# A two-layer sequence encoder on one core: weight sums and product adds pinned to traced order, PSUM banks dealt anew

## The chip, the core and the metric

The kernel runs on one core of a Trainium2 chip. Five engines of that core take part, each with its own in-order stream of instructions: TensorE (PE, matrix products, with its weight loads shown apart as PEld), VectorE (DVE), ScalarE (ACT), GpSimd (POOL) and SyncE (SP, which here only issues transfers). They meet through semaphores alone: an instruction whose operand isn't there holds up everything behind it on its engine. ACT has two jobs here: it computes, and it issues the transfers of the weight sums, from the same stream. Matrix products go to PSUM, eight banks of 128 partitions by 512 fp32 values.

The metric is the device time of one execution in microseconds (us); lower is better. Times of a comparison are medians of several runs.

## The reference

One sequence of 16 learned meta tokens and 256 frames, width 2048, goes through two post-norm layers:

```python
for layer in range(DEPTH):                       # DEPTH = 2
    f = _even_mixer(h, ...) if layer % 2 == 0 else _odd_mixer(h, ...)
    h = _layer_norm(DEEPNORM_ALPHA * h + f, ln_g[layer], ln_b[layer])
return h[:, PREFIX:]
```

The even mixer projects h (2048 wide) to queries, keys, values and gates of four gated-linear-attention (GLA) heads and eight stick-breaking attention heads, runs both, multiplies with SiLU gates and projects the 3072 columns back to 2048. The odd mixer is a Mamba-2 block: an input projection to z (4096), x (4096), B and C (1024 each) and 64 step sizes; a causal convolution of four taps and a SiLU on x, B, C; a scan in eight groups; an RMS norm per group of 512 columns; and the output projection of 4096 to 2048 columns. All weights and results are fp32.

## The kernel before

**Products.** Every large fp32 product is computed as three products of fp32r parts: a weight tile is split into whi (a rounding copy on ACT, line 191) and wlo (weight minus whi, a subtraction on DVE or sometimes POOL, line 192), and the activations into xhi and xlo. Lines 214, 215 and 216 are the three matmuls whi by xhi, whi by xlo and wlo by xhi.

**Units.** The weights are cut into units of 128 partitions by 2048 columns (1 MB), in the order of two lists, L0 (104 units of layer 0) and L1 (of layer 1). SP loads them into three buffers, raw. An input unit (in_unit) is 16 row blocks of three matmuls into one PSUM bank of the name pj, in four quarters of 12 matmuls; its result is then read out by a post function of its kind. In quarters 0 and 2 half of the next unit is split. Layer 0 goes through GLA heads 0 to 3, with output units between, then the two quads of stick-breaking heads. Layer 1 goes through the groups 0 to 7, each with the ten units B, C, x (four) and z (four). The first three units of layer 0 run interleaved while their data arrives; the ticks (below) begin after them.

**Side tasks.** Everything that isn't a unit is a Python generator: gates, transposes through DRAM, the mixers, the weight sums. After each quarter, tick() lets each waiting generator take one step. So the order in which the program is traced is the order of the units with the steps of the side tasks strewn in by ticks.

**Who sets the order on the chip.** The traced order is not the final one. A planner simulates the program and deals each engine its instructions: among those whose predecessors are through in its simulation, the one of highest priority, which follows the traced order, except that the post functions and some adds are traced with a high priority. It may thus issue an instruction much earlier than it stands in the trace, when its operands are there early. `keep_in_program_order` adds one edge: the instruction is issued behind the instruction that was traced just before it on its own engine. It is an edge of issue order, with no wait on a semaphore. Several matmul groups are pinned that way already; and the end of layer 0 and of the kernel are kept in traced order on DVE and ACT (keep_order).

**Weight sums.** The output projection of groups 0 to 5 in layer 1 uses a scheme of seven products of 2x2 blocks in place of eight (SEVEN). It needs four sums of weight blocks for each of 12 block sets, and these depend on weights alone, so they are computed during layer 0 by two generators (quad_sums, lines 560 to 582). Each of the 48 blocks of work loads 0.5 MB of weights into one of two buffers, quad (line 571, issued by ACT), lets 7 ticks pass, does four subtractions in place on DVE (line 575), lets 2 ticks pass, stores the result to DRAM (line 580, issued by ACT, tensor qs), and lets 4 ticks pass. The two generators start 12 and 19 ticks after the ticks begin and take every other block.

**Products of layer 1.** From quarter 72 of layer 1 on, 14 products per group are strewn between the quarters of the units (product, lines 615 to 637): six matmuls of 512 columns each (line 630) into one of two accumulator banks, then one add of the bank into acc on DVE (line 634). The add is put off to the next product_step, a quarter later. Its weights come through praw (SP) and lines 191 and 192. The products 0, 2, 4 and 6 of a set of seven use accumulator 0, the others accumulator 1.

**PSUM.** Eight banks: pj0 to pj3, po (two in rotation), z0 and z1. In layer 0 and the first six units of layer 1 the in-units rotate through all four pj banks; after that `self.pjs = (0, 1)`, and pj2 and pj3 are the product accumulators. z0 and z1 hold the score matrices of the mixers (zbank() deals them in turn), the means and scales of the first layer norm, and in layer 1 per group the small product cb of C and B (decay1, lines 1263 to 1274) and four small transposes (x_path). po serves short outputs: diagonal outputs of the scan (two), the mean square, x's transposes (two).

Of the kernel before, what the change touches and what calls it, by code (L numbers as in the profile page):

```python
# [117 lines left out]
class _Body:  # L118
# [114 lines left out]
    def run(self):  # L233
        tc, nc = self.tc, self.nc
        with tc.tile_pool(name="cp", bufs=1) as cp, tc.tile_pool(name="wp", bufs=1) as wp, tc.tile_pool(
            name="pp", bufs=1, space=PSUM
        ) as pp:
            self.cp, self.wp, self.pp = cp, wp, pp
            self.raw, self.parts = {}, {}
            self.zb = [pp.tile([P, 512], F32, tag=f"z{i}", name=f"z{i}") for i in range(2)]  # L240
            self.zi = 0

            self.dta = cp.tile([64, 2], F32, tag="dta", name="dta")
            self.b_one, self.b_rms, self.b_ln = [cp.tile([P, 1], F32, tag=n, name=n) for n in ("b_one", "b_rms", "b_ln")]
            self.xrows = [cp.tile([P, KT, XW], F32R, tag=n, name=n) for n in ("xhi", "xlo")]
            self.xhi, self.xlo = [x[:, :, X0 : X0 + T] for x in self.xrows]
            self.setup()
            with tc.tile_pool(name="hp", bufs=1) as hp:
                self.hp = hp
                a = hp.tile([P, HPG * 416], F32, tag="hacc", name="hacc")[:, : 12 * T].rearrange("p (k t) -> p k t", t=T)  # L250
                self.hacc = _TwoTiles(a, hp.tile([P, 4, T], F32, tag="hacc2", name="hacc2"))
                with tc.tile_pool(name="l0", bufs=1) as lp:
                    self.lp = lp
                    self.layer0()
                with tc.tile_pool(name="l1", bufs=1, reuse_waits="tile") as lp:
                    self.lp = lp
                    self.layer1()
# [301 lines left out]

    def quad_sums(self, start, first):  # L560

        nc, sub = self.nc, self.nc.vector.tensor_tensor
        for _ in range(start):
            yield
        for m in range(first, 8 * NS7, 2):
            g, q, c, x = m // 8, m // 4 % 2, m // 2 % 2, m % 2
            if (g, q) not in self.sums:
                self.sums[g, q] = self.tc.dram_tile([2, P, 2048], F32, name=self.nm("qs"))
            part = lambda a: a[c].rearrange("p (s x) -> p s x", s=4)[:, :, x * 256 : (x + 1) * 256]
            b = self.lp.tile([P, 4, 256], F32, tag="quad", name=self.nm("quad"), bufs=2)  # L570
            nc.scalar.dma_start(b, part(self.quad_rows(g, q)))
            for _ in range(7):
                yield
            for n, (o, u, v) in enumerate(((0, 1, 0), (1, 2, 1), (2, 2, 0), (3, 2, 3))):
                sub(b[:, o, :], b[:, u, :], b[:, v, :], op=ALU.subtract)  # L575
                if n % 2:
                    yield
            for _ in range(2):
                yield
            nc.scalar.dma_start(part(self.sums[g, q]), b)  # L580
            for _ in range(4):
                yield

# [31 lines left out]
    def product(self, k):  # L615

        mm = self.nc.tensor.matmul
        g, q, n = PRODUCTS[k]
        name, _, _, bank, first, (t, c) = SEVEN[n]
        while name not in self.left[g]:  # L620
            self.tick()
        yh, yl = self.left[g][name]
        hi, lo = [a.rearrange("p (k c) -> p k c", k=2) for a in self.pparts.pop(k)]
        if first and (n < 2):
            self.pbank[bank] = self.bank(2 + bank)
        ps = self.pbank[bank]
        f = first
        for j in range(2):
            for a, b in ((yh, hi), (yh, lo), (yl, hi)):
                mm(ps, a[:, j, :], b[:, j, :], start=f, stop=(j == 1 and a is yl), skip_group_check=True)  # L630
                f = False
        dq = 2 * q + c
        a = self.acc[:, t, dq * 512 : (dq + 1) * 512]
        self.padd = lambda: self.nc.vector.tensor_tensor(a, a, ps, op=ALU.add)  # L634
        self.pdone = k + 1
        self.product_load(k + 3)
        self.product_split(k + 1)
# [176 lines left out]

    def zbank(self):
        self.zi ^= 1
        return self.zb[self.zi]

    def mix_tile(self, g):
        lp = self.lp  # L820
# [229 lines left out]
    def layer1(self):  # L1050
        nc, lp = self.nc, self.lp
        self.acc = lp.tile([P, 2, D], F32, tag="acc", name="acc")
        self.praw, self.pparts, self.pbank = {}, {}, {}
        self.left_tiles = {n: [self.left_tile(a, k, t) for a in n] for n, k, t in LEFT}
        self.mt = lp.tile([16, HPG, 16], F32, tag="mt", name="mt")


        self.mt2 = lp.tile([48, 4, 2, 16], F32, tag="mt2", name="mt2")
        self.xd2 = lp.tile([48, 4, 64], F32, tag="xd2", name="xd2")
        nc.vector.memset(self.mt2, 0.0)  # L1060
        nc.vector.memset(self.xd2, 0.0)
        self.rstd1 = {}
        self.first1()
        self.pjs = (0, 1)
        self.units(len(L0), L1[:-5], {n: None for n in range(NFIRST)})
        self.tail()

# [156 lines left out]
    def decay1(self, g):  # L1224
        nc, lp = self.nc, self.lp
        act, vec, mm = nc.scalar.activation, nc.vector, nc.tensor.matmul
        bc = self.cur["bc", g]
        self.silu1(bc, None if g else vec)
        yield
        if g:  # L1230
            yield from _wait(*self.mixers[6 + g - 1])
        else:
            yield from _wait(self.tasks["dt"], self.tasks["res"])
            self.load_decay(0)
            yield
            yield
        if g > 1:
            bch, bcl = [a for a in lp.tile([P, 2, T + S], F32R, tag="gz", name=self.nm("bcp")).rearrange("p a c -> a p c")]
            act(bch, bc, AF.Copy)
            vec.tensor_tensor(bcl, bc, bch.bitcast(F32), op=ALU.subtract)  # L1240
            pairs = ((bch, bch), (bch, bcl), (bcl, bch))
        else:
            pairs = ((bc, bc),)

        M = lp.tile([P, HPG, 400], F32, tag="M", name=self.nm("M"))
        self.cur["M", g] = M
        eb = self.cur["ebc", g]
        for h in range(HPG):
            gh = g * HPG + h
            for s, c in ((0, slice(0, 256)), (1, slice(256, 400))):  # L1250
                act(M[:, h, c], eb[:, h, c], AF.Relu, bias=self.est[:, 0, s, gh : gh + 1], scale=-1.0)  # L1251
            if h % 2:
                act(M[:, h - 1 : h + 1, :], M[:, h - 1 : h + 1, :], AF.Exp, scale=-1.0)
                yield
        mt = self.mt
        e2 = self.est2[:, 0, g * HPG : (g + 1) * HPG].rearrange("p (h o) -> p h o", o=1).broadcast_to([16, HPG, 16])
        vec.tensor_tensor(mt, eb[:16, :, 400:416], e2, op=ALU.subtract)
        vec.tensor_scalar(mt, mt, 0.0, None, op0=ALU.min)
        act(mt, mt, AF.Exp)
        yield  # L1260

        for _ in range(2 if g else 0):
            yield
        zb = self.zbank()
        pin = self.tc.keep_in_program_order
        for o, s0, n, t0 in ((zb[:, 16:272], 0, P, 0), (zb[:, 272:416], P, P, 112), (zb[:16, 0:16], 2 * P, NM, 240)):
            for i, (b, c) in enumerate(pairs):
                pin(mm(o, b[:, s0 : s0 + n], c[:, T + t0 :], start=i == 0, stop=i == len(pairs) - 1))
        yield
        cb = lp.tile([P, 416], F32, tag="cb", name=self.nm("cb"))  # L1270
        act(cb, zb[:, :416], AF.Copy)
        self.causal(cb[:, 16:128], 112, False, 16)
        self.causal(cb[:, 272:400], 128, False)
        self.causal(cb[:16, 0:16], 16, False)
        yield
        for h in range(0, HPG, 2):
            c = cb[:, 16:416].rearrange("p (o c) -> p o c", o=1).broadcast_to([P, 2, 400])
            vec.tensor_tensor(M[:, h : h + 2, :], M[:, h : h + 2, :], c, op=ALU.mult)
            yield
        c = cb[:16, 0:16].rearrange("p (o c) -> p o c", o=1).broadcast_to([16, 2, 16])  # L1280
        m = mt.rearrange("s (p j i) t -> s j p i t", j=2, i=2)
        for j in range(2):
            for p in range(2):
                vec.tensor_tensor(self.mt2[32 * j : 32 * j + 16, 2 * p : 2 * p + 2, j, :], m[:, j, p], c, op=ALU.mult)
        yield
# [391 lines left out]
```

## Time and profile before

| what | value |
|---|---|
| time, median of 3 runs | 1498.27 us (1496.67 to 1498.56) |
| the profiled execution's own time | 1493.46 us |
| its span, first to last instruction | 1491.7 us |
| mean granted TensorE clock | 0.977 |
| PE, DVE, ACT, POOL busy | 94%, 76%, 56%, 18% |
| layer 0 | about 0 to 785 us |
| products of layer 1 | about 890 to 1415 us |

A row of the profile names line, engine, operation, output tile <- input tiles, count, and busy time with the mean of one. A row of a view of waits says which engine and line waited for which engine (or DMA) and line, how many us in total, how many times and the longest. PEclk or "clock" is the share of full clock that TensorE was granted. Idle time of an engine that isn't the bottleneck costs nothing by itself.

### The profile page before, as it was taken

To read this page: it belongs to the slowest core of one execution; us is meant where nothing else is said; L and a number is where in the kernel's file an instruction comes from. 1 tells how busy PE (TensorE), PEld (TensorE's weight loads), DVE (VectorE), ACT (ScalarE), POOL (GpSimd) and SP (SyncE) were. 2 spreads that over 40 slices of the span, in tenths; PEclk is the share of its full clock that TensorE was granted. 3 is DMA by queue.
4 is the path that set the end of the run, shared out by engine and by line. 5 is a ranking of instruction groups with operands and counts; after the bars stand their busy time and mean duration, and the time that the engine had idled before them with its cause. 6 is when DMAs were issued, how large, how long until landed. Compare 5 with 4: busy or idle time off the path is not lost.

```text
span 1491.7 us, 26723 instructions
## 1 busy us (share of the span) xinstructions
PE 1399.3 (94%) x10559; PEld 1335.1 (89%) x10559; DVE 1137.7 (76%) x1924; ACT 842.8 (56%) x1299; POOL 269.4 (18%) x269
## 2 busy tenths in 40 slices
PE   6898979989989999999998989999999999999998
PEld 6798979989988999999998989888988989988986
DVE  5867658678667567456888877987879798787977
ACT  4444424434434554455568777668675776858661
POOL 0001000000000110001610131233224223222241
PEclk8899998999999999999999999999999999999999
DMA  9778877887986545554535647666576666756551
GB/s 313 245 262 274 266 252 236 289 284 261 304 273 210 177 158 181 177 175 157 170 141 188 232 174 244 226 214 243 184 250 214 227 233 215 240 179 229 187 198 57
DMA packets 132029, 325.97 MB, mean 219 GB/s; under 512 B 28672, under 2 KB 80704, under 8 KB 106560
## 3 DMA queue, kind: packets, MB, share of 16 engines
q1 hardware_dynamic: 80496, 273.15, 54.2%
q10 hardware_dynamic: 51408, 51.12, 10.3%
q8 instruction: 83, 1.36, 0.4%
q14 instruction: 42, 0.34, 0.1%
HBM read 293.33 MB, written 30.91 MB: 217 GB/s over the span
## 4 chain that ended last, share of the span: by engine, by line
PE 57%; DMA 16%; DVE 16%; issue 5%; ACT 5%; POOL 1%; ACTq 1%; DVEq 0%; SPq 0%; POOLq 0%
PE pj L214 15%; PE pj L216 15%; PE pj L215 15%; DMA qs<-quad 7%; DMA quad<-in_wts 6%; DVE wlo L192 6%; PE pj L630 5%; DVE quad L575 2%; ACT whi L191 2%; PE po L1435 1%; DMA raw<-in_wts 1%; ACT M L1251 1%; DVE xt L1195 1%; DVE acc L634 1%; PE po L754 1%
## 5 line engine op out<-in xcount | busy, mean ns | idle before, releaser
L214 PE MATMUL pj<-xhi,whi 128*128 128x272 f32 (+4 forms) x2560 | 740.0, 290 | 14.9 <-DVE bc L1195 5.6
L215 PE MATMUL pj<-xlo,whi 128*128 128x272 f32 (+4 forms) x2560 | 736.9, 288 | 7.0 <-DVE xlo L369 6.8
L216 PE MATMUL pj<-xhi,wlo 128*128 128x272 f32 (+4 forms) x2560 | 735.9, 288 | 5.3 <-DVE wlo L192 5.1
L191 ACT ACTIVATE whi<-raw 128x1024 fp32r<-128x1024 f32 (+2 forms) x386 | 395.4, 1033 | 315.6 <-PE pj L215 162.6
L192 DVE TENSOR_TENSOR wlo<-raw,whi 128x1024 fp32r<-128x1024 f32 (+2 forms) x365 | 443.4, 1220 | 156.4 <-ACT whi L191 155.4
L214 PEld LDWEIGHTS pj<-xhi,whi 128*128 128x128 f32 x2560 | 487.5, 191 | 24.8 <-issue 7.7
L215 PEld LDWEIGHTS pj<-xlo,whi 128*128 128x128 f32 x2560 | 487.9, 191 | 11.6 <-DVE xlo L369 7.0
L216 PEld LDWEIGHTS pj<-xhi,wlo 128*128 128x128 f32 x2560 | 488.3, 191 | 6.7 <-DVE wlo L192 5.9
L575 DVE TENSOR_TENSOR quad<-quad 128x256 f32<-128x256 f32 x192 | 85.5, 460 | 49.7 <-DMA quad<-in_wts 48.4
L214 PE MATMUL pj<-mixh,whi 128*128 128x272 f32 x384 | 114.9, 300 | 3.7 <-DVE hacc L489 2.7
L192 DVE TENSOR_TENSOR wlo<-praw,whi 128x1024 fp32r<-128x1024 f32 x84 | 110.3, 1314 | 8.1 <-ACT whi L191 8.0
L215 PE MATMUL pj<-mixl,whi 128*128 128x272 f32 x384 | 113.5, 296 | 0.0
L216 PE MATMUL pj<-mixh,wlo 128*128 128x272 f32 x384 | 113.1, 295 | 0.0
L191 ACT ACTIVATE whi<-praw 128x1024 fp32r<-128x1024 f32 x84 | 88.5, 1053 | 30.8 <-PE pj L215 17.1
L634 DVE TENSOR_TENSOR acc<-acc,pj 128x512 f32<-128x512 f32 x84 | 57.1, 679 | 38.7 <-PE pj L630 38.6
L214 PEld LDWEIGHTS pj<-mixh,whi 128*128 128x128 f32 x384 | 75.4, 197 | 4.9 <-DVE hacc L489 3.4
L299 POOL TENSOR_TENSOR gr<-gr,gsc 128x1088 f32<-128x1088 f32 x6 | 16.3, 2724 | 346.8 <-ACT gsc L298 259.6
L215 PEld LDWEIGHTS pj<-mixl,whi 128*128 128x128 f32 x384 | 75.6, 197 | 0.2
L216 PEld LDWEIGHTS pj<-mixh,wlo 128*128 128x128 f32 x384 | 75.4, 196 | 0.0
L192 POOL TENSOR_TENSOR wlo<-raw,whi 128x1024 fp32r<-128x1024 f32 x21 | 56.2, 2674 | 99.3 <-ACT whi L191 99.3
L1251 ACT ACTIVATE M<-ebc,est 128x256 f32<-128x256 f32 (+1 forms) x128 | 46.1, 448 | 19.3 <-PE po L1435 18.9
L1206 POOL TENSOR_TENSOR gz<-gz,xcl 128x512 f32<-128x512 f32 x16 | 27.2, 1703 | 110.9 <-ACT xcl L1205 96.5
(395 smaller groups left out, 1781.0 us busy)
## 6 DMA issues: line engine op xcount, KB each, us to landing
raw<-in_wts SPq DMA_DIRECT2D x188, 1024.0 KB, 5.7
quad<-in_wts ACTq DMA_DIRECT2D x48, 512.0 KB, 6.5
qs<-quad ACTq DMA_DIRECT2D x48, 512.0 KB, 6.0
praw<-qs SPq DMA_DIRECT2D x48, 512.0 KB, 4.1
praw<-in_wts SPq DMA_DIRECT2D x36, 512.0 KB, 4.2
ebc<-edr SPq DMA_DIRECT2D x8, 1664.0 KB, 6.7
raw<-in_wts SPq DMA_DIRECT2D x9, 256.0 KB, 7.4
vdr<-vt SPq DMA_DIRECT2D x8, 256.0 KB, 4.1
```

The costliest lines, as they stand in the source:

```text
L191: self.nc.scalar.activation(hi, src, AF.Copy)
L192: eng.tensor_tensor(lo, src, hi.bitcast(F32), op=ALU.subtract)
L214: mm(ps, whi, xhi, start=first, stop=False)
L215: mm(ps, whi, xlo, start=False, stop=False)
L216: mm(ps, wlo, xhi, start=False, stop=last)
L299: mul(c, c, e, op=ALU.mult)
L575: sub(b[:, o, :], b[:, u, :], b[:, v, :], op=ALU.subtract)
L630: mm(ps, a[:, j, :], b[:, j, :], start=f, stop=(j == 1 and a is yl), skip_group_check=True)
L634: self.padd = lambda: self.nc.vector.tensor_tensor(a, a, ps, op=ALU.add)
L754: mm = lambda r, a, b, start=False, stop=False: self.nc.tensor.matmul(o[:, r], a, b, start=start, stop=stop, skip_group_check=True)
L1206: (eng or self.nc.gpsimd).tensor_tensor(v, v, c, op=ALU.mult)
L1251: act(M[:, h, c], eb[:, h, c], AF.Relu, bias=self.est[:, 0, s, gh : gh + 1], scale=-1.0)
```

## The change

Four things, all of order and place; no arithmetic changes.

1. In quad_sums, the load, the four subtractions and the store of each block are pinned with `keep_in_program_order`: loads and stores behind the instruction traced before them on ACT, subtractions behind the one traced before them on DVE.
2. After the first units of layer 1 the in-units rotate through pj0, pj1 and pj2. Accumulator 0 of the products moves from pj2 to z1, and zbank() deals only z0 from then on.
3. cb takes a po bank instead of a z bank. Its copy to SBUF is split in two (columns 16 to 415 of all partitions, columns 0 to 15 of 16 partitions), because a po bank isn't zeroed where cb isn't written.
4. The products' adds into acc are pinned behind the instruction traced before them on DVE.

```diff
@@ run
-            self.zi = 0
+            self.zi, self.two_z = 0, True
@@ quad_sums
-        nc, sub = self.nc, self.nc.vector.tensor_tensor
+        nc, sub, pin = self.nc, self.nc.vector.tensor_tensor, self.tc.keep_in_program_order
...
-            nc.scalar.dma_start(b, part(self.quad_rows(g, q)))
+            pin(nc.scalar.dma_start(b, part(self.quad_rows(g, q))))
             for _ in range(7):
                 yield
             for n, (o, u, v) in enumerate(((0, 1, 0), (1, 2, 1), (2, 2, 0), (3, 2, 3))):
-                sub(b[:, o, :], b[:, u, :], b[:, v, :], op=ALU.subtract)
+                pin(sub(b[:, o, :], b[:, u, :], b[:, v, :], op=ALU.subtract))
                 if n % 2:
                     yield
             for _ in range(2):
                 yield
-            nc.scalar.dma_start(part(self.sums[g, q]), b)
+            pin(nc.scalar.dma_start(part(self.sums[g, q]), b))
@@ product
-            self.pbank[bank] = self.bank(2 + bank)
+            self.pbank[bank] = self.bank(3) if bank else self.zb[1]
...
-        self.padd = lambda: self.nc.vector.tensor_tensor(a, a, ps, op=ALU.add)
+        self.padd = lambda: self.tc.keep_in_program_order(self.nc.vector.tensor_tensor(a, a, ps, op=ALU.add))
@@ zbank
-        return self.zb[self.zi]
+        return self.zb[self.zi if self.two_z else 0]
@@ layer1
-        self.pjs = (0, 1)
+        self.pjs, self.two_z = (0, 1, 2), False
@@ decay1
-        zb = self.zbank()
+        zb = self.po()
...
-        act(cb, zb[:, :416], AF.Copy)
+        act(cb[:, 16:], zb[:, 16:416], AF.Copy)
+        act(cb[:16, :16], zb[:16, :16], AF.Copy)
```

## The prediction

> **What bounds the kernel now.** I read the busy time by stage first, then what TensorE (PE) waited for in each stage, then the group of the weight sums, then a stretch of the timeline. The table has the stretch, its length, busy time and count of each engine, granted clock, DMA share and GB/s.
>
> ```profile
> 0.00:25.00 25.00, 15.48 (x98) 15.05 (x99) 16.01 (x55) 9.22 (x18) 1.83 (x14) 0.86 0.88 285
> 25.00:500.00 475.00, 428.88 (x3280) 419.71 (x3279) 336.82 (x663) 202.64 (x291) 27.42 (x29) 0.95 0.79 263
> 500.00:785.00 285.00, 285.00 (x2301) 283.67 (x2301) 193.23 (x325) 150.11 (x239) 47.57 (x76) 1.00 0.50 166
> ...
> 900.00:1400.00 500.00, 480.93 (x3570) 445.86 (x3570) 424.24 (x587) 350.58 (x525) 148.09 (x114) 1.00 0.66 224
> ...
> sum 1492.00, PE 1399.34 PEld 1335.08 DVE 1137.73 ACT 842.82 POOL 269.43; mean PE 233.22 PEld 222.51 DVE 189.62 ACT 140.47 POOL 44.90
> ```
>
> PE is the bound on average, busy 1399 of 1492 us, and the stages differ. From 500 to 785 us PE never stops: 285 us / 2301 = 123.9 ns per matmul. At that pace the 3280 matmuls of 25 to 500 us need 406 us; they take 475. So 69 us are lost there: 475 - 428.9 = 46 us idle, and the other 23 us at a reduced clock (0.95 of 429 us is 21 us). Layer 1 from 900 to 1400 loses 19 us. So the first 500 us hold most of what can be won.
>
> What sets those first 500 us apart is the weight sums (tile quad): their rows end at 465 us.
>
> ```profile
> L575 DVE TENSOR_TENSOR quad<-quad x192: 381/419/2766, 10.5 to 464.9; 128x256 f32<-128x256 f32 x192
> L571 ACTq DMA_DIRECT2D quad<-in_wts x48: 547/600/857, 4.8 to 457.6; - x48
> ...
>   ACT whi L191: 79.0, 18
>   DVE quad L575: 48.4, 22
>   ACT xhi L368: 6.7, 1
>   ACT gsq L858: 6.0, 1
>   ACT ga L662: 5.6, 2
>   ACT qe L684: 5.2, 2
>   ACT spad L843: 4.6, 1
> ```
>
> The first load is issued at 4.8 us, though the code asks for it 12 ticks after the first three units. Under it stands who waited for these transfers and sums: DVE 48.4 us for loads, ACT 107.1 us by the rows shown, for sums or for a store to land (the load of the next block sits on ACT's queue until the store that empties its buffer is through). ACT's largest row divides so:
>
> ```profile
> ACT whi L191 <- DMA qs<-quad: 44.9, 10, 8.0
> ...
> ACT whi L191 <- DVE quad L575: 34.2, 8, 5.9
> ```
>
> With gsq and qe, which waited for stores, 56 us are on stores and 51 on sums. One such place, around 430 us:
>
> ```profile
> 427.69 1.06 ACT L191 ACTIVATE whi<-raw 128x1024 fp32r<-128x1024 f32 x1 [4.44 <-DMA qs<-quad]
> 428.74 0.89 DVE L575 TENSOR_TENSOR quad<-quad 128x256 f32<-128x256 f32 x2 [4.04 <-DMA quad<-in_wts]
> 429.54 0.43 DVE L811 TENSOR_TENSOR gk<-pj,ke 128x272 f32<-128x272 f32 x1
> ...
> 430.03 0.50 PE L836 MATMUL z<-gq,gk 128*128 128x272 f32 x1 [1.91 <-DVE gk L811]
> ```
>
> ACT stands 4.44 us for a store, DVE 4.04 us for a load; gk queues behind the sum, and PE waits for gk. The chain is: DMA, in-order DVE or ACT, PE.
>
> **The change, part by part.** (1) The sums' 48 loads, 192 subtractions and 48 stores are pinned. They are the same instructions, so no busy time is added; only their places change. A pin puts each behind the instruction traced before it on its own engine, so the planner can no longer float them to the front; each stream of blocks now paces itself by ticks. One block has 15 ticks: 7 from load to first subtraction, 2 through the four subtractions, 2 to the store, 4 to the next load. A tick in microseconds comes from the chain's start and end of the first layer's ticks:
>
> ```profile
> 35.92 1.96 PE pj L397 x28
> ...
> 785.76 4.05 ACT hacc L1122 x8
> ```
>
> 101 units of four ticks in about 749 us is 1.85 us per tick. So the load gets 13 us, and the store 7.4 us before the next load wants its buffer. Against that stand the landings:
>
> ```profile
> quad<-in_wts ACTq DMA_DIRECT2D x48, 512.0 KB, 6.5
> qs<-quad ACTq DMA_DIRECT2D x48, 512.0 KB, 6.0
> ```
>
> The loads have 6.5 us to spare, the stores 1.4 us. The sums then run to tick 379 or so, near 740 us, instead of 465.
>
> What PE's waits before 500 us are worth:
>
> ```profile
> PE z L836 <- DVE gk L811: 18.1, 6, 5.3
> PE pj L215 <- DVE xlo L369: 6.8, 1, 6.8
> PE po L754 <- ACT gsq L858: 5.9, 2, 4.9
> ...
> PE po L868 <- ACT s0h L695: 3.4, 2, 1.8
> ...
> PE po L661 <- DVE gm L663: 2.3, 1, 2.3
> ...
> PE po L661 <- ACT gsq L858: 2.0, 1, 2.0
> PE po L869 <- DVE s0l L696: 1.2, 1, 1.2
> ```
>
> I looked at each wait's place as at 430 us. Behind gk, the early xlo (ACT stood 6.7 us for a sum), both gsq rows, s0h, s0l and gm stands a transfer or sum of quad: 18.1 + 6.8 + 5.9 + 2.0 + 3.4 + 1.2 + 2.3 = 39.7 us. I leave the other rows out; there DVE and ACT were simply full. The 23 us of lost clock follow PE's idleness: all of the 39.7 us but the xlo row lie after 25 us, 32.9 of the 46 idle us there, so 16.5 us of the clock belong to the sums. The ceiling of (1) is 56.2 us.
>
> How much of it is realized is my main choice. Lower end: a pin is tied to one predecessor only, and where that is a weight split (whi or wlo), which the planner runs up to a unit (4 ticks) ahead, the slack shrinks from 7 ticks to 3, or from 4 to none; then a quarter is won, 14 us. Upper end: all. By the waits themselves: those on loads and sums are 48.4 + 51 us, those on stores 56. If all of the first and half of the second go, 82% of 156 us does. I take 65%, for the loose pins: **37 us**. The 35% left counts all 48 blocks, also the 17 or so that move into 500 to 740 us, where no PE wait hides today; their 4 x 0.42 us of subtractions fit DVE's 92 idle us there.
>
> A sentence on the clock by a page: the Trainium skill, "TensorE: Matmul & The Clock Gate", section "What's actually happening", has the clock halved after an idle window of some 3.4 us, and restored after a busy one as long. By that rule the single stalls above 3.4 us (xlo and the longest gk and gsq) make the loss, and shortening them to 2 us would give back all 23 us of clock, which would add some 12 us to my 65%. The trace's 0.86 and 0.95 beside 1.00 in the stretch without stalls agree in direction; I keep the scaling.
>
> (2) Three banks for layer 1's in-units instead of two. PE's waits there:
>
> ```profile
> PE pj L214 <- DVE bc L1195: 5.6, 5, 1.2
> PE pj L630 <- DVE wlo L192: 4.8, 3, 1.6
> ...
> PE pj L214 <- ACT gz L1347: 2.5, 2, 1.8
> ...
> PE pj L214 <- DVE xt L1195: 0.7, 3, 0.3
> ```
>
> The bc, gz and xt rows are an in-unit's first matmul that waits until the unit before last has left its bank: 8.8 us. With a third bank the unit gets one more unit's length. I take **7 us** (from 0, if the planner spends the freedom elsewhere, to 8.8).
>
> (3) The product's first accumulator moves to a z bank, and cb to the two po banks. In trace order a group takes po for the diagonal outputs at tick 4, the mean square at 12, now cb at 20, the transposes at 33; each is read out some 8 ticks before its bank comes up again. Nothing, as long as that holds; cb's copy becomes two:
>
> ```profile
> L1271 ACT ACTIVATE cb<-z x8: 497/500/520, 832.2 to 1398.6; 128x416 f32<-128x416 f32 x8
> ```
>
> Eight more copies of 16x16, each under the 0.5 us of this one, under 4 us on an ACT that idles 150 of 500 us: 0 (up to 4 if each stood in PE's way).
>
> (4) The products' adds pinned, one quarter of a unit after their product.
>
> ```profile
> L634 DVE TENSOR_TENSOR acc<-acc,pj x84: 666/680/689, 900.9 to 1413.4; 128x512 f32<-128x512 f32 x84
> ...
>   PE pj L630: 38.6, 20
> ```
>
> Today 20 of 84 adds sit at DVE's head before their product is done, 38.6 us in all, with weight splits queued behind them. That idleness goes; of PE's waits only the wlo row (4.8 us, a product that waits for its split) follows from it. Bounds: 4.8 won; 8 lost, if the first product of each of the 12 sets of seven had to wait for one add of 0.68 us. I take **1 us**, near the middle on the side of the row that exists.
>
> Sum: 37 + 7 + 0 + 1 = 45 us. The profiled execution took 1493.5 us (its span and 1.8 around it), the median of the runs is 1498.3, 4.8 more. So 1448.5 by the profile, and **1453 us** for the runs.
>
> **Rivals.** *The waits mostly stay* (A). The faster PE goes, the shorter a tick: 12 matmuls at 123.9 ns are 1.5 us, and 4 ticks 5.9 us, just the store's 6.0; with loads floating behind early splits, ACT goes on standing for stores. For it: 56 us of ACT's waits are on stores. Against it: a slower pace of blocks (15 ticks, 28 us, instead of 19 us in the mean by the rows 4.8 to 457.6 for 24 pairs) leaves the DMA less full. A quarter of 56.2 is 14, with 4 from the banks: 18 us, 1480.
>
> The Trainium skill, "DMA: Bandwidth & Descriptors", section "Anatomy of one DMA — SWDGE (gpsimd) path", says that a wait ahead of a DMA is spent on the issuing sequencer, and that the receipt of a write to HBM can come surprisingly late. It speaks for A: a pin moves a store's wait, it does not take it off ACT's queue. The trace's 6.0 us agrees; pages and rows give A the same 1480.
>
> *Late adds* (B), the slower side. With a third bank PE no longer stops for DVE, and a pinned add is behind whatever DVE has ahead. The tightest reuse is a seventh product's bank by the next set's first, 3 quarters later, 2 after the add. A group takes
>
> ```profile
> 917.44 2.86 PE po L1435 x32
> 1006.08 2.86 PE po L1435 x32
> ```
>
> 88.6 us for 40 quarters, so 2 quarters are 4.4 us. 12 sets wait for what DVE is late beyond that. At 9 us late this is 12 x 4.6 = 55 us, 10 more than the gain: 1508; it decides from 8.2 us on (12 x 3.8 = 45). For it: DVE is busy 424 of 500 us. Against it: PE's longest wait for DVE there is 1.6 us.
>
> *Nothing moves* (C): the predecessors are themselves hoisted, and the order stays: 1498. Against it: the first loads at 4.8 us would have to pass a predecessor in the seventh unit.
>
> **Chances.** Forecast, 1428 to 1470: 0.59. A, 1470 to 1493: 0.26. B: 0.10. C: 0.05. A measurement here tells 0.2% (3 us) from no change, so: faster 0.85 (forecast and A), same 0.05 (C), slower 0.10 (B). The low end is 56.2 + 8.8 + 4.8 = 70 us, 1428; the high end takes in A, 1491.
>
> **What would show it.** Right: the sums' rows begin near 50 us and end near 740; ACT's and DVE's waits on quad fall from 156 us to some 55; gk as a cause of PE's waits under 6 us; clock above 0.98; 25 to 500 us with over 3550 matmuls; in layer 1 no bc or gz wait, adds' idle before them under 10 us. Wrong: rows of waits on store landings as large as now; PE waits on quad's victims after 500 us; PE's L630 waiting for acc L634.

## The result and the profile after

The changed kernel takes 1435.0 us (median of 4 runs, 1426.4 to 1438.7) against 1498.4 us before (4 runs). The ratio is 0.9566, 95% interval 0.9519 to 0.9612: 63 us faster by the medians, where 45 us were forecast. In a later group of runs on one chip the ratio of the same two kernels was 0.9627 (0.9580 to 0.9674), so the size is known to about half a per cent. The profiled executions stand at 1434.4 and 1493.5 us, 59 us apart; the working below goes by these two.

The stages, in the same stretches as before (length, busy time and count of PE, PEld, DVE, ACT, POOL, granted clock, DMA share, GB/s), of the changed kernel:

```profile
0.00:25.00 25.00, 22.55 (x162) 22.34 (x163) 19.15 (x55) 16.17 (x27) 1.83 (x14) 1.00 0.92 326
25.00:500.00 475.00, 459.56 (x3674) 454.97 (x3672) 354.49 (x673) 224.53 (x327) 32.25 (x44) 0.99 0.76 254
500.00:785.00 285.00, 277.06 (x2231) 273.70 (x2231) 225.60 (x407) 162.46 (x267) 41.83 (x61) 1.00 0.64 213
...
900.00:1400.00 500.00, 487.93 (x3589) 452.77 (x3589) 444.43 (x599) 343.96 (x520) 166.64 (x117) 1.00 0.65 219
```

From 25 to 500 us PE now does 3674 matmuls where it did 3280; the clock went from 0.95 to 0.99, and the first 25 us hold 162 matmuls in place of 98, at full clock. The stretch from 500 us on, which never stopped before, now has small gaps (8 us). Of these 5.4 us lie ahead of 735 us, where PE waits for s0h and ke (small copies on ACT that feed PE) behind transfers and subtractions of the sums, which now reach into this stretch; the other 2.5 us belong to the first units of layer 1, which now begin before 785 us.

As the mark for the end of layer 0 I take the last start in one row, the scaling of the normalized rows. It stands once per kernel; here before, then after:

```profile
L1122 ACT ACTIVATE hacc<-hacc,cpk x16: 599/600/604, 780.2 to 789.2; 128x272 f32<-128x272 f32 x16
```

```profile
L1122 ACT ACTIVATE hacc<-hacc,cpk x16: 597/600/604, 730.4 to 739.4; 128x272 f32<-128x272 f32 x16
```

Layer 0 ends 49.8 us earlier (789.2 to 739.4). What comes after it takes 1432.6 - 739.4 = 693.2 us in place of 1491.7 - 789.2 = 702.5: 9.3 us. Together these are the 59 us.

The group of the weight sums after the change, and what PE waited for before 500 us:

```profile
L575 DVE TENSOR_TENSOR quad<-quad x192: 382/419/2760, 52.0 to 657.0; 128x256 f32<-128x256 f32 x192
L571 ACTq DMA_DIRECT2D quad<-in_wts x48: 547/547/666, 37.6 to 631.5; - x48
L580 ACTq DMA_DIRECT2D qs<-quad x48: 569/570/646, 60.4 to 663.5; - x48
...
  ACT whi L191: 65.0, 18
...
  DVE quad L575: 26.5, 13
...
DMA to landing us min/median/max: 3.3/5.8/13.2
```

```profile
PE po L754 <- ACT s0h L695: 5.0, 2, 4.7
PE pj L216 <- DVE wlo L192: 3.4, 1, 3.4
PE z L836 <- DVE gk L811: 3.3, 2, 1.8
PE z L914 <- ACT ke L889: 2.8, 1, 2.8
```

The first load goes out at 37.6 us and not at 4.8, the last store at 663.5. PE's waits for gk fell from 18.1 to 3.3 us; the xlo wait of the start and both gsq rows are gone. The longest wait that is left shows its cause in the timeline:

```profile
280.93 0.55 ACTq L571 DMA_DIRECT2D quad<-in_wts  x1
281.52 0.53 ACT L843 ACTIVATE spad<-z 128x432 f32<-128x432 f32 x1 [10.68 <-DMA qs<-quad]
...
283.50 0.39 PE L754 MATMUL po<-s0h,gvh 128*128 128x272 f32 x1 [4.73 <-ACT s0h L695]
```

A load of the sums stands on ACT until a store has landed; spad (a copy of scores on ACT) and s0h wait behind it for 10.68 us, and PE for 4.73. ACT's waits split so (rows of the first 740 us):

```profile
ACT whi L191 <- DMA qs<-quad: 46.7, 12, 8.2
...
ACT whi L191 <- DVE quad L575: 14.5, 5, 4.0
ACT spad L843 <- DMA qs<-quad: 10.7, 1, 10.7
ACT s0h L695 <- DMA qs<-quad: 4.8, 1, 4.8
ACT sbe L924 <- DMA qs<-quad: 3.8, 1, 3.8
ACT ke L889 <- DVE quad L575: 3.7, 1, 3.7
ACT v L740 <- DMA qs<-quad: 3.4, 1, 3.4
```

With two rows of 1.3 and 1.1 us, ACT stood 72 us for stores: more than the 56 us before. It stood 18 us for subtractions (51 before), and DVE 26.5 us for loads (48.4 before). A second profile of the changed kernel has 86, 17 and 24 us, so the 72 is known to some 15 us only.

### The profile page after: what moved, and what is told of

Its sections match the earlier page's. It is cut to its first block, busy times and chain, and to the rows that moved or that the text cites. A ratio compares the mean times of both kernels' runs of the same rounds, so it can differ in the third digit from the quotient of the medians.

```text
span 1432.6 us, 26754 instructions
## 1 busy us (share of the span) xinstructions
PE 1380.2 (96%) x10559; PEld 1321.8 (92%) x10559; DVE 1157.4 (81%) x1924; ACT 841.6 (59%) x1307; POOL 278.0 (19%) x269
## 4 chain that ended last, share of the span: by engine, by line
PE 62%; DVE 15%; DMA 14%; ACT 4%; issue 4%; SPq 1%; ACTq 0%; POOL 0%; DVEq 0%; POOLq 0%
PE pj L216 16%; PE pj L214 16%; PE pj L215 16%; DMA qs<-quad 6%; DVE wlo L192 5%; PE z L630 4%; DMA quad<-in_wts 3%; PE pj L630 3%; DVE quad L575 2%; ACT whi L191 2%; PE po L1436 1%; DMA vdr<-vt 1%; DVE M L1279 1%; DMA vt<-vdr 1%; PE po L754 1%
## 5 line engine op out<-in xcount | busy, mean ns | idle before, releaser
L192 DVE TENSOR_TENSOR wlo<-raw,whi 128x1024 fp32r<-128x1024 f32 (+2 forms) x365 | 453.8, 1249 | 125.2 <-ACT whi L191 123.6
L192 DVE TENSOR_TENSOR wlo<-praw,whi 128x1024 fp32r<-128x1024 f32 x84 | 114.2, 1359 | 19.4 <-ACT whi L191 18.6
L214 PE MATMUL pj<-mixh,whi 128*128 128x272 f32 x384 | 111.3, 291 | 0.0
L575 DVE TENSOR_TENSOR quad<-quad 128x256 f32<-128x256 f32 x192 | 86.8, 455 | 28.3 <-DMA quad<-in_wts 26.5
L299 POOL TENSOR_TENSOR gr<-gr,gsc 128x1088 f32<-128x1088 f32 x6 | 15.6, 2592 | 331.4 <-ACT gsc L298 297.1
L1203 ACT ACTIVATE xcl<-xcl 128x544 f32<-128x544 f32 (+2 forms) x40 | 25.2, 640 | 35.2 <-DVE xcl L1202 35.1
```

Source lines behind the costliest of these rows:

```text
L192: eng.tensor_tensor(lo, src, hi.bitcast(F32), op=ALU.subtract)
L214: mm(ps, whi, xhi, start=first, stop=False)
L299: mul(c, c, e, op=ALU.mult)
L575: pin(sub(b[:, o, :], b[:, u, :], b[:, v, :], op=ALU.subtract))
L1203: act(c, c, AF.Exp, scale=-1.0)
```

## The experiments

All ratios are against the kernel before, timed beside it. "Layer 0 end" is the last start in the row shown above; "rest" is the span from there on; both are read from one profiled execution of each kernel.

| kernel | ratio, 95% interval | layer 0 end, us | rest, us |
|---|---|---|---|
| before | 1 | 789.2 | 702.5 |
| changed | 0.9566 (0.9519 to 0.9612) | 739.4 | 693.2 |
| sums pinned alone | 0.9691 (0.9656 to 0.9726) | 743.9 | 705.8 |
| banks alone | 0.9938 (0.9912 to 0.9964) | 790.9 | 695.8 |
| adds pinned alone | 0.9997 (0.9975 to 1.0019) | 792.5 | 702.2 |
| changed, no weight sums | 0.9462 (0.9436 to 0.9488) | 715.7 | 696.0 |
| changed, subtractions unpinned | 0.9631 (0.9573 to 0.9689) | 752.9 | 696.0 |
| changed, transfers unpinned | 0.9673 (0.9634 to 0.9713) | 745.1 | 698.6 |
| changed, ticks moved to the store | 0.9620 (0.9582 to 0.9658) | 742.0 | 699.3 |
| changed, sums' loads on SP | 0.9513 (0.9476 to 0.9551) | 719.7 | 697.1 |
| changed, once more | 0.9627 (0.9580 to 0.9674) | 737.1 | 696.0 |
| changed, adds unpinned | 0.9610 (0.9569 to 0.9652) | 739.6 | 692.8 |
| changed, two in-unit banks | 0.9663 (0.9622 to 0.9704) | 735.8 | 704.4 |
| changed, loads on SP, sums unpinned | 0.9713 (0.9669 to 0.9758) | 753.9 | 693.3 |

The kernels came in three groups of four, each on one chip: the first four experiments, the next four, and the last four. The changed kernel's 0.9566 is from a measurement of its own; its 0.9627 is beside the last four. Medians under half a per cent apart are not told apart here, and a stage moves by a few us between profiles: layer 0 of the changed kernel ended at 739.4 and 737.1, and the rest of kernels that differ in layer 0 alone took 693 to 699 us. Four of the profiled executions were the longest of their kernel: sums alone (1451.5 us, median 1445.7), banks alone (1488.4, median 1482.6), subtractions unpinned (1450.7, median 1438.0) and ticks moved (1443.0, median 1437.5). Their two last columns are that much less typical.

**Each part alone.**

```diff
@@ sums_only: the kernel before, and
+            pin(nc.scalar.dma_start(b, part(self.quad_rows(g, q))))
+                pin(sub(b[:, o, :], b[:, u, :], b[:, v, :], op=ALU.subtract))
+            pin(nc.scalar.dma_start(part(self.sums[g, q]), b))
```

> The kernel before with only the loads, subtractions and stores of the weight sums pinned; banks and adds as before. Theory (the layer-0 gain of 50 us between the two profiles is the pins on the sums, by shorter waits of ACT and DVE): layer 0 ends near 736 us, ratio 0.965 (about 1446 us), layer 1 as before (706 us long). Rival (the gain needs the new banks too, because the planner lays the whole program anew): layer 0 ends later than 750 us, ratio above 0.975.

Measured: 0.9691, layer 0 ends at 743.9 us, the rest is about as before (705.8 and 702.5). The theory holds: the pins on the sums alone bring 45 of the 50 us of layer 0, and nothing in layer 1. The interval (0.9656 to 0.9726) does not reach the rival's 0.975.

```diff
@@ banks_only: the kernel before, and
+            self.pbank[bank] = self.bank(3) if bank else self.zb[1]
+        self.pjs, self.two_z = (0, 1, 2), False
+        zb = self.po()
+        act(cb[:, 16:], zb[:, 16:416], AF.Copy)
+        act(cb[:16, :16], zb[:16, :16], AF.Copy)
```

> The kernel before with only the bank changes (three in-unit banks, accumulator 0 on z1, cb on po in two copies); nothing newly pinned. Theory: layer 0 as before (785 us), layer 1 shorter by the bank waits of 8.8 us: 697 to 700 us long, ratio 0.994 to 0.996. Rival (the 9 us of layer 1 come from the pinned adds, or from the planner): ratio 0.998 to 1.004.

Measured: 0.9938, layer 0 as before, the rest 6.7 us shorter. That is the theory's, at the edge of its range. PE's waits of in-units for bc, gz and xt are gone from its view; what grew is a wait for a weight split, which a bank can't cure:

```profile
PE pj L216 <- DVE wlo L192: 10.5, 5, 2.7
PE pj L214 <- ACT whi L191: 3.7, 2, 2.6
```

```diff
@@ adds_only: the kernel before, and
-        self.padd = lambda: self.nc.vector.tensor_tensor(a, a, ps, op=ALU.add)
+        self.padd = lambda: self.tc.keep_in_program_order(self.nc.vector.tensor_tensor(a, a, ps, op=ALU.add))
```

> The kernel before with only the products' adds pinned. Theory: DVE's 38.6 us of waits ahead of the adds fall under 15 us, but PE gains at most the 4.8 us it waited for wlo: ratio 0.997 to 1.001. Rival (DVE's idleness was holding PE up throughout layer 1): ratio 0.990 to 0.995. Late adds, the slower rival of the prediction: ratio above 1.003 and PE rows waiting for the add.

Measured: 0.9997 (0.9975 to 1.0019): no difference. DVE's waits ahead of the adds fell only to 21.5 us, not under 15. PE's wlo wait halved, but PE now waits for adds, and for gz in place of bc:

```profile
PE pj L214 <- ACT gz L1347: 9.3, 7, 1.8
...
PE pj L630 <- DVE acc L634: 4.3, 7, 1.1
PE pj L630 <- DVE wlo L192: 2.4, 5, 1.0
```

So late adds do exist, with two banks at 4.3 us in all; they were never near the price that would have turned the result. With three banks they cost 2.9 us in the changed kernel (2.2 and 0.7).

The three ratios multiply to 0.9628, the changed kernel's own in the last group (0.9627): within the noise the parts add up, and nothing is left for their acting together.

**What the sums cost in all.**

```diff
@@ no_sums: the changed kernel, and
-        for n in range(2):
-            self.push(self.quad_sums(12 + 7 * n, n))
-        src = self.sums[g, q] if is_sum else self.quad_rows(g, q)
+        src = self.quad_rows(g, q)
```

> The changed kernel without the weight sums: their loads, subtractions and stores are left out, and the products read unsummed weight blocks in their place, so the output is not the reference's. It prices what the sums still cost. Theory (the pins took off most of the 56 us ceiling): layer 0 ends only 4 to 10 us earlier than 736, and the time is 5 to 10 us below the changed kernel's. Rival (the waits mostly stayed and something else gave the gain): layer 0 ends 20 us or more earlier, below 716 us.

Measured: 0.9462, and layer 0 ends here:

```profile
L1120 ACT ACTIVATE hacc<-hacc,cpk x16: 599/601/604, 706.8 to 715.7; 128x272 f32<-128x272 f32 x16
```

That is 23.7 us earlier than the changed kernel, and neither theory named it: mine said 4 to 10, the rival took 20 or more for a sign that the gain had another cause. It hasn't, for the sums alone bring it; the two statements of the rival don't belong together. The price of the sums in the kernel before was not 56 us but 789.2 - 715.7 = 73.5; the pins took off 49.8 of them, 68%. Without sums PE waits before 715 us for two things only, the constants at the start and one weight split:

```profile
PE pj L216 <- DVE wlo L192: 3.4, 1, 3.4
PE po L278 <- DVE ones_r L273: 2.3, 1, 2.3
```

**Which pins.**

```diff
@@ dma_pins: the changed kernel, and
-                pin(sub(b[:, o, :], b[:, u, :], b[:, v, :], op=ALU.subtract))
+                sub(b[:, o, :], b[:, u, :], b[:, v, :], op=ALU.subtract)
```

> The changed kernel with the subtractions unpinned; loads and stores of the sums stay pinned. Theory (the stalls come through the transfers: a load sent early waits on ACT for a store, and subtractions cannot run before their load): nearly all of the gain stays, ratio 0.955 to 0.965, layer 0 ends within 8 us of 739, but DVE waits more for loads than the 26.5 us of the changed kernel. Rival (DVE's place for the subtractions is what counts): layer 0 ends after 760 us, ratio above 0.970.

```diff
@@ sub_pins: the changed kernel, and
-            pin(nc.scalar.dma_start(b, part(self.quad_rows(g, q))))
+            nc.scalar.dma_start(b, part(self.quad_rows(g, q)))
-            pin(nc.scalar.dma_start(part(self.sums[g, q]), b))
+            nc.scalar.dma_start(part(self.sums[g, q]), b)
```

> The changed kernel with loads and stores unpinned; the subtractions stay pinned. Theory: two buffers and pinned subtractions already pace the blocks, so the stores cannot run far ahead; but each load goes out as soon as its buffer is empty and stands on ACT for the store. ACT's waits on store landings rise above the 61 us of the changed kernel, and part of the gain is lost: ratio 0.960 to 0.975. Rival (pinned subtractions alone do it): ratio 0.952 to 0.960, waits on stores no larger.

Measured: 0.9631 with the transfers pinned, 0.9673 with the subtractions pinned. Either half holds most of the gain; a likely reason is that with two buffers each paces the other. Which half is worth more isn't settled, the intervals overlap. With free subtractions DVE waits 76.3 us for loads (26.5 with the pin), as expected; probably the planner puts them where it believes the load to have landed. Layer 0 was to end within 8 us of 739 and ends at 752.9, 13.5 later; as this profile is 13 us above its kernel's median, the miss is not shown to be the kernel's. With free transfers my number missed: ACT's waits on stores did not rise (68 us by the rows, 72 in the changed kernel; the 61 us of the expectation left some rows out), though the first load goes out at 4.6 us again; its waits for subtractions rose, from 18 to 35.

**Is it the stores on ACT's queue?**

```diff
@@ slack_store: the changed kernel, and
-            for _ in range(7):
+            for _ in range(4):
...
-            for _ in range(4):
+            for _ in range(7):
```

The first of the two loops lies between load and first subtraction, the second between store and next load.

> The changed kernel with three of the seven ticks between load and first subtraction moved behind the store: 4, 2, 2, 7 in place of 7, 2, 2, 4. The period of a block stays 15 ticks. Theory (what is left of the sums' price, 24 us by the kernel without sums, is ACT standing for store landings): ACT's waits on stores fall from 61 us below 25, DVE's waits on loads rise from 26.5 us to 35 to 60; layer 0 ends 3 to 12 us earlier than 739, ratio 0.948 to 0.955. Rival (what is left is loads that come too late for their subtractions): layer 0 ends later than 742 us, ratio above 0.960.

Measured: 0.9620, layer 0 ends at 742.0. The waits did what the theory said, ACT stood 25 us for stores in place of 72, and DVE 37.6 us for loads:

```profile
  DMA quad<-in_wts: 37.6, 16
...
  ACT whi L191: 43.2, 12
  DVE quad L575: 37.6, 16
```

The time did not follow; it came out as the rival had it (742 us, above 0.960). DVE's and ACT's waits together fell from 116 to 85 us. PE's idle time from 25 to 500 us fell too, by 2 us, but the clock of this profile is lower (the changed kernel has 459.56 us, 3674 matmuls and 0.99):

```profile
25.00:500.00 475.00, 461.56 (x3650) 456.95 (x3650) 354.51 (x671) 223.28 (x325) 33.49 (x41) 0.97 0.76 253
```

The lower clock is not shown to come from the moved ticks. The profiled execution had a mean clock of 0.981, the three others of this kernel 0.987 to 0.989, and six of the changed kernel in the last group 0.984 to 0.989. From 45 to 60 us PE has one and the same wait in several of the profiles, 3.4 us for wlo, and the clock behind it still differs. Here are the changed kernel, this one and the one without sums:

```profile
45.00:60.00 15.00, 11.57 (x81) 11.35 (x80) 11.98 (x34) 4.15 (x10) 0.00 (x0) 0.89 0.66 216
```

```profile
45.00:60.00 15.00, 11.57 (x71) 11.35 (x70) 11.68 (x33) 4.25 (x10) 0.00 (x0) 0.77 0.68 217
```

```profile
45.00:60.00 15.00, 11.57 (x73) 11.35 (x72) 9.68 (x29) 4.14 (x10) 0.00 (x0) 0.77 0.55 175
```

The same wait was followed by 8 to 10 matmuls fewer, over 1 us, in the second and the third, and the third is the fastest kernel of all. What the ratio does show is that 31 us less of named waits brought no measurable time, so the theory of that run falls in the form it had. A stronger cut was needed.

```diff
@@ sp_loads: the changed kernel, and
-            pin(nc.scalar.dma_start(b, part(self.quad_rows(g, q))))
+            pin(nc.sync.dma_start(b, part(self.quad_rows(g, q))))
```

> The changed kernel with the loads of the sums issued by SP instead of ACT, pinned there behind SP's instruction traced before. The stores stay on ACT. Theory (ACT loses by standing for a store ahead of the next load): ACT's waits on store landings go to near 0, layer 0 ends 5 to 15 us earlier than 739, ratio 0.946 to 0.953. Rival (SP then stands for the store, and the weight loads queue behind it, or a load queues behind a weight load that waits for its buffer): PE or ACT waits for raw, layer 0 no earlier than 735, ratio 0.955 or more.

Measured: 0.9513 (0.9476 to 0.9551), 1421.0 us, the lowest ratio of the kernels that compute the sums. Against the changed kernel's 0.9627 of the last group the intervals are apart; against its first 0.9566 they meet. Its layer 0 ends earlier than the 724 to 734 us that were expected, near that of the kernel without sums:

```profile
L1122 ACT ACTIVATE hacc<-hacc,cpk x16: 598/601/605, 710.8 to 719.7; 128x272 f32<-128x272 f32 x16
```

```profile
  DVE quad L575: 17.4, 13
  ACT whi L191: 13.7, 5
```

```profile
SPq L571 <- DMA qs<-quad: 147.6, 34, 9.2
SPq L176 <- DVE wlo L192: 105.3, 29, 10.8
```

ACT has no wait on a store left; its only row on the sums is 13.7 us for subtractions. The waits for stores have not vanished: SP now stands 148 us for them. Behind it are weight loads, most of which wait for their buffers anyway, and the transposes through DRAM. Some of the rival's price is there (ACT's waits for raw are 10.2 us where the two profiles of the changed kernel have 4.0 and 6.3, for gvh's transposes 32.1 where they have 26.2 and 17.2), but no wait of PE shows it. Of the 23.7 us that the sums still cost, this takes off 19.7 (739.4 to 719.7).

```diff
@@ sp_unpinned: loads on SP as above, and
-                pin(sub(b[:, o, :], b[:, u, :], b[:, v, :], op=ALU.subtract))
+                sub(b[:, o, :], b[:, u, :], b[:, v, :], op=ALU.subtract)
-            pin(nc.scalar.dma_start(part(self.sums[g, q]), b))
+            nc.scalar.dma_start(part(self.sums[g, q]), b)
```

> The changed kernel with the sums' loads on SP and none of the sums' instructions pinned; adds still pinned. Theory (two causes: the planner sends the sums too early, into the start, and ACT stands for stores): the second cause is gone, the first stays, so layer 0 ends between 735 and 765 us with the xlo wait of some 7 us at the start; ratio 0.960 to 0.980. Rival (only the queue mattered): layer 0 ends near 720, ratio below 0.955.

Measured: 0.9713, layer 0 ends at 753.9, within the theory. The sums run early again (subtractions from 27.3 to 441.9 us), and their victims are back:

```profile
  DVE quad L575: 66.0, 30
  ACT whi L191: 57.0, 13
  ACT ga L662: 11.4, 3
```

```profile
PE z L836 <- DVE gk L811: 12.7, 4, 5.7
```

Only the xlo wait at the start did not come back, which the theory had expected. That does not clear the bandwidth that early sums take, for SP sends the first load only at 19.2 us. The kernel with its transfers unpinned says more: its two first loads go out at 4.6 and 5.7 us, its subtractions late, and it has no xlo wait either. So that wait came through ACT's stream (in the kernel before, xhi stands behind a store that waits for an early subtraction). But its first 25 us hold 131 matmuls, half way between 98 before and 162 after:

```profile
0.00:25.00 25.00, 21.22 (x131) 20.46 (x132) 16.48 (x52) 13.27 (x24) 1.83 (x14) 0.93 0.87 283
```

What cost the 31 is not taken apart. So two things move layer 0's end: sums placed before their data is there (the pins are worth 50 us with loads on ACT, 789.2 to 739.4, and 34 us with loads on SP, 753.9 to 719.7), and loads that stand on ACT for a store (35 us without pins, 789.2 to 753.9; 20 us with them, 739.4 to 719.7). The two overlap: together they bring 69.5 us, some 16 less than the two alone would add up to.

**Layer 1 once more.**

> The changed kernel once more, as the anchor of this group of runs on one chip. Theory: ratio 0.954 to 0.962.

Measured: 0.9627, 1437.1 us (6 runs, 1433 to 1449), at the upper edge of what was expected and just past it.

```diff
@@ no_add_pin: the changed kernel, and
-        self.padd = lambda: self.tc.keep_in_program_order(self.nc.vector.tensor_tensor(a, a, ps, op=ALU.add))
+        self.padd = lambda: self.nc.vector.tensor_tensor(a, a, ps, op=ALU.add)
```

> The changed kernel with the products' adds unpinned. Theory (with three in-unit banks the pin lets DVE run on instead of standing for products, and PE's wlo waits shorten from 10.5 us, as in the kernel with banks alone, to 3.6): layer 1 is 2 to 4 us longer than the changed kernel's 693, ratio higher than the changed kernel's by 0.001 to 0.004. Rival (the pin does nothing, as alone): no difference, within 0.001. Late adds: ratio lower by 0.002 or more.

```diff
@@ two_banks: the changed kernel, and
-        self.pjs, self.two_z = (0, 1, 2), False
+        self.pjs, self.two_z = (0, 1), False
```

> The changed kernel with the in-units of layer 1 on two banks again (pj0, pj1); accumulators, cb and all pins as changed. Theory (the third bank is what the bank change is worth): PE waits for gz, bc and xt come back with 8 to 13 us, layer 1 is 6 to 10 us longer than 693, ratio 0.004 to 0.007 above the changed kernel's. Rival (cb off the z banks, or the accumulator's place, gave it): within 0.002 of the changed kernel.

Measured: without the add pin 0.9610, the rest 692.8 us: no difference from the changed kernel that can be told (0.0017 below it, with intervals of 0.004 to each side), and nothing for my theory of 2 to 4 us more. DVE stands 31.8 us for products (15.6 with the pin), PE 9.1 us for wlo (3.6 with it), and neither shows at the end. With two banks 0.9663, 8 us above the changed kernel of its group by the medians, though the intervals overlap; the rest is 704.4 us in place of 696.0, and the waits for banks are back:

```profile
PE pj L214 <- ACT gz L1348: 9.3, 7, 1.8
PE pj L214 <- DVE xt L1195: 5.1, 4, 3.1
```

The table agrees: the four kernels with two in-unit banks have a rest of 702.2 to 705.8 us, the ten with three 692.8 to 699.3. The third bank is thus layer 1's gain as far as these runs can tell; the accumulator on z1 and cb on po are only what pays for it.

## Why the prediction was right, and where a size was off

*The bound and the mechanism* held. PE's lost time in the first 500 us came from the sums, through ACT and DVE, and the pins on the sums alone give 45 us of layer 0.

*The ceiling of 56.2 us* was mis-sized: it measured 73.5. The step that failed is "I leave the other rows out; there DVE and ACT were simply full". In the kernel without sums the rows for whi, hacc, vt, shiftc and xhi (9.6 us before) are gone with the rest; only wlo's stays, 3.4 us for 4.2, which was rightly left out. And all of the 23 us of clock belonged to the sums, not 16.5: the 3813 matmuls that the kernel without sums does from 25 to 500 us take 124 ns each, as in the stretch without stalls. These two, 9.6 and 6.5 us, are most of the 17.3 us that the ceiling lacked. (By the full view ACT's waits before were 57.5 us for stores and 52.6 for sums; the prediction's 56 and 51 left out one row of 3.0 us and put 1.4 us for a store with the sums.)

*The share of 65%* was near: 49.8 of 73.5 is 68%. But the reason given for it was wrong, so that it came near is luck; of the prediction's own 56.2 us the gain is 89%. I had let the load's waits vanish and half of the stores' go. Loads and subtractions went from 99 to 45 us; the stores' went up, from 56 to 72. Rival A named this mechanism (a tick shrinks as PE speeds up; 594 us from the first load to the last are 352 ticks, some 1.69 us each and not 1.85, so 4 ticks are some 6.7 us against the median landing of a store below). The median fits in that; ACT stood for the later ones, 18 times. By the kernel with loads on SP this is what holds back the last 20 us. It did not decide, because most of the old loss lay on the other side.

```profile
qs<-quad ACTq DMA_DIRECT2D x48, 512.0 KB, 6.2
```

*The clock.* My scaling was mis-sized. The clock of 25 to 500 us is 0.99, some 5 us lost of 460, so 18 of the 23 us came back, not 11. These 7 us are more than half of the 13 that (1) brought beyond the forecast 37. The sentence by the rule of the Trainium skill ("TensorE: Matmul & The Clock Gate", "What's actually happening") came nearer in size, but the trace agrees with that rule only in part. Two stalls over 3.4 us are left (4.73 and 3.43), and a fall of the clock follows each; yet the clock stood at half also behind the stall of 2.82 us at 447.96:

```profile
448.00:451.00 3.00, 3.00 (x13) 3.00 (x14) 2.55 (x3) 0.85 (x1) 0.00 (x0) 0.50 0.91 355
```

In the second profile of the changed kernel it did so behind a stall of 1.98 us (0.50 from 596 to 598 us). With the rows from 45 to 60 us above, where equal stalls cost unequal clock, no sum by the length of stalls is exact here.

*The third bank*, 7 us: measured 6.7 alone and 8 as the last step. *cb and the accumulator* at nothing: nothing can be seen; cb's second copy takes 0.156 us each time, and PE's waits in layer 1 show one for a po bank, 1.2 us at its start, where it was 1.1 before. *The adds*, 1 us: nothing, within the bounds given.

```profile
L1272 ACT ACTIVATE cb<-po x8: 154/156/158, 796.5 to 1339.1; 16x16 f32<-16x16 f32 x8
```

*The signs to look for*: the sums begin at 37.6 us (near 50 was said) and end at 663 (740: the tick was too long); gk 3.3 us (under 6); clock 0.991 (above 0.98); 3674 matmuls (over 3550); adds' idle 15.6 us (under 10 was said); no bc or gz wait is left in layer 1, only 2.2 us for xt. ACT's and DVE's waits on quad fell to 116 us where some 55 were said. Of the signs set down as "wrong", store waits as large as now came true in full, and shows where the rest lies. The other two came true in small: 5.4 us of PE's waits on quad's victims after 500 us, and 2.9 us of L630 waiting for L634.

*Rivals.* B, late adds, cost 2.9 us where 45 were needed. C, that nothing moves, is excluded by the rows of the sums.

## What to carry to other kernels

Look at which in-order engine issues a transfer that must first wait for another transfer. Here these waits cost some 20 us on ACT, which computes, and nothing that PE's waits show on SP, which only issues. An order dealt out by a simulation can send early whatever has no predecessor; one edge of issue order per instruction, tied to work of the right time, won 50 of the 73.5 us back here. Price a suspect by leaving it out: a count of waits with its name on them missed a quarter of what the sums cost, and cutting the count of waits by a quarter (116 to 85 us) brought nothing. And ask how typical a profiled execution is of its kernel's runs before explaining a few us by its clock.

## What was not expected of the hardware

- The landing of a 0.5 MB transfer is widely spread: 3.3 to 13.2 us with a median of 5.8 in the changed kernel, while the DMA engines' mean share was 0.76 from 25 to 500 us. One of the long ones, in the chain of waits, made the longest stall of layer 0 after the start:

```profile
267.75 13.16 DMA qs<-quad
```

- Two of the subtractions, 0.42 us each by the median, took 3.22 us together while a product of GpSimd on 1088 columns ran (the changed kernel):

```profile
441.60 2.57 POOL L299 TENSOR_TENSOR gr<-gr,gsc 128x1088 f32<-128x1088 f32 x1 [44.42 <-ACT gsc L298]
441.69 3.22 DVE L575 TENSOR_TENSOR quad<-quad 128x256 f32<-128x256 f32 x2
```

  The store behind them came late, then whi and ke on ACT, and PE stood 2.82 us at 447.96. The same stands in nine profiles of kernels that compute the sums: every subtraction that took over 1 us by the timeline (2.1 to 2.8 us where it stands alone) ran beside such a product. That the two engines hold each other up is an inference from the times; no run here takes it apart.
- The clock does not follow the length of a stall alone: behind the same wait of 3.4 us it was 0.89 or 0.77 from 45 to 60 us, and it stood at half behind waits of 2.82 and 1.98 us. What decides it stays open.
